# A two-layer RWKV-7 and S5 trunk: the bonus product is written over the receptance, and both pairs' bonus sums share one PSUM bank

## The chip, the cores and the metric

The kernel runs on one core of a Trainium2 chip. The metric is the device time of one execution in microseconds (us), as the median of the runs. The engines are named as in the profile: PE (matrix products), DVE (vector), ACT (scalar), POOL (GpSimd) and SP, which issues most of the DMAs.

## What is computed

The reference is a trunk of two layers over x of 1 x 1024 steps x 1024 features, float32. The first layer is RWKV-7 time mixing, the second an S5 state-space layer with a gated output; each is followed by a squared-ReLU MLP, and a LayerNorm stands after every part. The change lies in the first layer alone:

```python
r, k, v = xr @ wr, xk @ wk, xv @ wv
kk = k * k_k                      # per head, scaled to length 1
k = k * (1.0 + (a - 1.0) * k_a)
# per step of a head: state (64 x 64), decay w, o = state @ r
state = state * w + (state @ -kk) (kk * a)^T + v k^T
o = groupnorm(o) * lnx_g + lnx_b
bonus = sum(r * k * r_k, axis=-1) * v
out = ((o + bonus) * g) @ wo
```

The bonus is one number for each step and head, the sum over the head's 64 features of receptance times key times a weight `r_k`, by which the value `v` is scaled. There are 16 heads of 64 features.

## The kernel before

**Dense products.** The projections, the output product and the MLPs are written as three products of a high and a low part each (`mm3`, L257), with weights that stream from memory (L216 and L224 are their loads, L192 and L193 the split into parts). They take most of PE's time. Those of the second half of the steps and of the output run on PE between the products of the RWKV units.

**Units.** The recurrence is done in eight units of 256 steps and 512 features (8 heads), unit m in `elem(m)`. A unit has two pairs, j = 0 and 1, of two tiles of 128 features each. The steps form chunks of 64.

`elem` loads for a pair the key, the log decay `sg`, the rate `a` and the receptance `r` from DRAM scratch (L594; tiles `ldk`, `ldsg`, `lda`, `ldr`, each with two buffers, so that one pair's load takes the buffer that the same pair of the unit before has used). It sums squares for the norms (pss, L616, a power on POOL, a copy L621, transposes pn, L624, then the multiply into kk), runs a scan over `sg` (L629) and its exponentials E, builds the key `kf` (L638, L640; one buffer) and, on DVE, the operands of the unit's score products: AR from `r` and E (L643) and from kk (L644), KB from `kf`, `a` and `sg` (L648, L649).

Then POOL multiplies `kf` by `r` in place (L650). `bonus` takes four small products of it with the weights (pb, L654), in a bank of its own of the PSUM pool `pa`, and copies the sums out with two copies on DVE and two on ACT (L661). The pool `pa` has two banks, which hold pss, pn, the score blocks pA and the sums in turn. For j = 0 the sums stand behind the transposes pn of j = 1, for j = 1 behind the unit's last score product; an explicit order (`inorder`, L247) says so.

`amat` computes the score matrix in four blocks of eight products (pA, L687), each block in both banks of `pa`, and moves each to SBUF with a mask (AT, L691). `kbtrans` transposes KB (L702), `invert` inverts the chunk matrices (xa, x, xh, pv; L724 to L753, on DVE and PE by turns), `chain` runs the recurrence chunk by chunk (pR L796, its copy L798, pX L801, the copies to `vsa` on DVE L802 and ACT L803, pU L806, state L809 and L810, pO L815 and L817), and `gnorm` makes the output, with the copied sums `bo` as the bonus.

**Order.** The program is ordered by a list scheduler. Each part gets a rank (`core`), the scheduler has its own estimates of durations, and engines then run their instructions strictly in the order that comes out; while unit m runs its chain, unit m+1 runs `elem`, `amat` and `invert`. An instruction starts when the semaphores that it waits for are there, and everything behind it on its engine waits as well. A DMA issue on SP behaves in the same way.

Of the kernel before, what the change touches and what calls it, by code (L numbers as in the profile page):

```python
# [8 lines left out]
F32 = mybir.dt.float32  # L9
# [9 lines left out]
HT = 512  # L19
# [61 lines left out]
def trunk(ctx, tc, A):  # L81
    nc = tc.nc
    V, S, G, PE, SP = nc.vector, nc.scalar, nc.gpsimd, nc.tensor, nc.sync
# [8 lines left out]
    pa = ctx.enter_context(tc.tile_pool(name="pa", bufs=2, space=PSUM))  # L92
# [14 lines left out]
    ident = cp.tile([128, 128], F32, name="ident")  # L107
# [15 lines left out]
    def vec(n, k):  # L123
        i = PV.index(n)
        return pv[:, i, k : k + 1]
# [7 lines left out]
    rksel = kp.tile([128, KT, 2], F32, name="rksel")  # L133
# [113 lines left out]
    def inorder(prods):  # L247

        for x, y in zip(prods, prods[1:]):
            tc.add_manual_dep(y.ins, x.ins.name, mybir.DependencyInfo(  # L250
                mybir.DependencyClass.NoSync, mybir.DependencyReason.DATA), reason="order")
# [323 lines left out]
    NC, NP = 4, 4  # L575
# [7 lines left out]
    def elem(m):  # L583
        D = Unit()
        D.m, D.H, D.q, D.t0 = m, m // 4, m % 2, (m // 2) * 256
        D.KB, D.AR, D.o, D.vsa = [], [], {}, {}
        D.bo = kp.tile([128, NC, NP], F32, tag="bo", name="bo", bufs=3)
        D.PL = kp.tile([128, NC, NP], F32, tag="PL", name="PL", bufs=3)
        for j in range(2):
            n0 = 4 * D.q + 2 * j  # L590
            ld = {}
            for nm in ("k", "sg", "a", "r"):
                t = kp.tile([128, 512], F32, tag="ld" + nm, name="ld" + nm, bufs=EB[3] if nm in EB[4] else 1)
                SP.dma_start(t.rearrange("p (i t) -> p i t", i=2),  # L594
                             scr[nm][n0 * 128 : n0 * 128 + 256, D.t0 : D.t0 + 256].rearrange("(i p) t -> p i t", p=128))
                ld[nm] = t
            r, k, cs, a = ld["r"], ld["k"], ld["sg"], ld["a"]

            def v3(t):
                return t.rearrange("p (c l) -> p c l", l=L)  # L600

            def per(i):
                return slice(256 * i, 256 * i + 256)

            def ci(t):
                return t[:, :, 2 * j : 2 * j + 2].rearrange("p c i -> p i c")


            sq = kp.tile([128, HT], F32, tag="sq", name="sq", bufs=EB[0])
            kk = kp.tile([128, HT], F32, tag="kk", name="kk", bufs=EB[1])  # L610
            for i in range(2):
                S.mul(kk[:, per(i)], k[:, per(i)], vec("k_k", n0 + i))
            S.activation(sq, kk, AF.Square)
            ps = pa.tile([128, HT], F32, tag="a", name="pss")
            for tt in range(4):
                PE.matmul(ps[:, tt * 2 : tt * 2 + 2], sq[:, tt * 128 : (tt + 1) * 128], hsel, start=True, stop=True)  # L616
            rn = kp.tile([128, 8], F32, tag="rn", name="rn", bufs=2)
            V.tensor_scalar(rn, ps[:, 0:8], 1e-24, None, op0=ALU.max)
            G.tensor_tensor(rn, rn, mhalf[:, 0:8], op=ALU.pow)
            rnb = sq.rearrange("p (t h n) -> p t h n", t=4, h=2)  # L620
            S.copy(rnb, rn.rearrange("p (t h) -> p t h", h=2).unsqueeze(3).broadcast_to([128, 4, 2, 64]))  # L621
            pn = pa.tile([128, HT], F32, tag="a", name="pn")
            for tt in range(4):
                last = PE.transpose(pn[:, tt * 128 : (tt + 1) * 128], sq[:, tt * 128 : (tt + 1) * 128], ident)  # L624
            if j:
                D.bonus(last)
            V.tensor_mul(kk, kk, pn)

            V.tensor_tensor_scan(cs, cmask.rearrange("p c l -> p (c l)"), cs, 0.0, op0=ALU.mult, op1=ALU.add)  # L629
            E = kp.tile([128, 8, L + 1], F32, tag="E", name="E", bufs=EB[5])  # L630
            G.memset(E[:, :, 0:1], 1.0)
            S.activation(E[:, :, 1:], v3(cs), AF.Exp, scale=-DECAY)
            V.tensor_copy(ci(D.PL), E[:, :, L].rearrange("p (i c) -> p i c", i=2))
            S.activation(cs, cs, AF.Exp, scale=DECAY)

            kf = kp.tile([128, HT], F32, tag="kf", name="kf", bufs=EB[2])
            for i in range(2):
                S.activation(kf[:, per(i)], a[:, per(i)], AF.Identity, bias=kam[:, n0 + i : n0 + i + 1],  # L638
                             scale=kah[:, n0 + i : n0 + i + 1])
            G.tensor_mul(kf, kf, k)  # L640
            ar = kp.tile([128, 8, 2, L], F32, tag="AR", name="AR", bufs=ARB)
            kb = kp.tile([128, 8, 2, L], F32, tag="KB", name="KB", bufs=KBB)
            V.tensor_mul(ar[:, :, 1], v3(r), E[:, :, 1:])  # L643
            V.scalar_tensor_tensor(ar[:, :, 0], v3(kk), -1.0, E[:, :, 0:L], op0=ALU.mult, op1=ALU.mult)  # L644
            V.scalar_tensor_tensor(a, a, 1.0, kk, op0=ALU.add, op1=ALU.mult)
            for h in range(2):
                hs = slice(64 * h, 64 * h + 64)
                V.tensor_mul(kb[hs, :, 1 - h], v3(kf)[hs], v3(cs)[hs])  # L648
                V.scalar_tensor_tensor(kb[hs, :, h], v3(a)[hs], 0.5, v3(cs)[hs], op0=ALU.mult, op1=ALU.mult)  # L649
            G.tensor_mul(kf, kf, r)  # L650
            def bonus(after, kf=kf, n0=n0, j=j):
                pb = pa.tile([128, HT], F32, tag="a", name="pb")
                for tt in range(4):
                    prod = PE.matmul(pb[:, 2 * tt : 2 * tt + 2], kf[:, tt * 128 : (tt + 1) * 128], rksel[:, n0 + tt // 2],  # L654
                                     start=True, stop=True)
                    if tt == 0:
                        inorder([after, prod])
                pbv = pb[:, 0:8].rearrange("p (i c h) -> p c i h", i=2, c=2)
                for h in range(2):
                    for e in range(2):  # L660
                        (V.tensor_copy if e == 1 - h else S.copy)(  # L661
                            D.bo[64 * (1 - h) : 64 * (1 - h) + 64, e::2, 2 * j : 2 * j + 2],
                            pbv[64 * e : 64 * e + 64, :, :, h])

            D.bonus = bonus
            D.KB.append(kb)
            D.AR.append(ar)
        return D

    def amat(D):  # L670
# [7 lines left out]
        for j in range(2):  # L678
            for c2 in range(2):
                pp = [pa.tile([128, 2, 2, 128], F32, tag="a", name="pA") for h in range(2)]  # L680
                prods = []
# [8 lines left out]
                for h in range(2):  # L690
                    V.tensor_mul(at[:, h, 2 * c2 : 2 * c2 + 2, 2 * j : 2 * j + 2].rearrange("p c i j l -> p c i (j l)"),  # L691
                                 pp[h], amask.rearrange("p u j l -> p u (j l)").unsqueeze(1).broadcast_to([128, 2, 2, 128]))
        D.bonus(prods[-1])

    def kbtrans(D):
        D.kbt = {}
# [186 lines left out]
    def core():  # L883
# [6 lines left out]
        with rank(3000):  # L890
            cur = elem(0)
        with rank(5000):
            amat(cur)
            invert(cur)
# [800 lines left out]
    with rank(99100):  # L1695
        for k in range(4):
            a = t1[k]
# [104 lines left out]
```

## Time and profile before

| what | value |
|---|---|
| median of 3 runs | 2534.3 us (2532.02 to 2540.27) |
| profiled execution, device time | 2528.45 us |
| profiled execution, span of the trace | 2526.7 us |
| mean granted PE clock | 0.982 of full |
| POOL busy | 411.1 us (16%) |
| DMA, mean over the span | 135 GB/s |

The profile is that of one execution. Busy time is given for each engine; the chain of waits goes back from the last instruction to whatever released it; a row of a wait reads "engine, tile, line <- releaser: total, count, longest". The RWKV units run from about 75 to about 900 us of the span; the S5 layer and the MLPs fill the rest. POOL is the least busy of the engines in the table.

### The profile page before, as it was taken

The page shows a single profiled execution, that of the slowest core. Times are in us where ns is not written, and L with a number is a line of the kernel's source. Part 1 is how long each engine was busy: PE and PEld are TensorE (multiplying, and loading weights), DVE is VectorE, ACT ScalarE, POOL GpSimd, SP SyncE. Part 2 cuts the span into 40 slices and gives each one's busy share as a digit, 9 for nine tenths or more (in the row PEclk, how much of TensorE's full clock was granted, in tenths as well). Part 3 has the DMA queues.
Part 4 walks back from the last instruction along what each step waited for, and adds up shares of the span by engine and source line. Part 5 has one row for each costly group of instructions (what it writes and reads, how often), then busy time and mean ns, then how long its engine had stood idle before and what let it go on. Part 6 is the DMA issues. An engine that isn't in the chain of part 4 may idle for free.

```text
span 2526.7 us, 43006 instructions
## 1 busy us (share of the span) xinstructions
PE 2444.8 (97%) x16320; PEld 1996.6 (79%) x16320; DVE 1711.1 (68%) x3309; ACT 1217.3 (48%) x2197; POOL 411.1 (16%) x334
## 2 busy tenths in 40 slices
PE   9999889899899999999999999999999999999998
PEld 6788677688777878777788887887878888888887
DVE  7578787488795655997656475677666555655555
ACT  7655666454554444265445444434464333343434
POOL 3122332232231001021000000100232111111101
PEclk9999999999899999999999999999999999999998
DMA  5966555664223224444456565254351111111233
GB/s 177 311 214 206 166 188 159 209 185 132 70 78 97 90 84 147 130 132 119 131 178 192 170 248 187 92 190 144 114 170 58 54 48 55 47 54 51 87 112 114
DMA packets 217678, 340.60 MB, mean 135 GB/s; under 512 B 21248, under 2 KB 81792, under 8 KB 217472
## 3 DMA queue, kind: packets, MB, share of 16 engines
q1 hardware_dynamic: 216320, 335.77, 42.1%
q8 instruction: 128, 2.10, 0.4%
q10 hardware_dynamic: 1152, 2.10, 0.2%
q14 instruction: 78, 0.64, 0.1%
HBM read 267.53 MB, written 70.25 MB: 134 GB/s over the span
## 4 chain that ended last, share of the span: by engine, by line
PE 82%; DVE 8%; DMA 5%; ACT 3%; issue 1%; SPq 0%; POOL 0%; ACTq 0%; DVEq 0%; POOLq 0%
PE d L257 62%; PE d L1228 10%; PE pA L687 1%; DMA ldsg<-s_sg 1%; PE pk L1460 1%; DMA yl<-s_y 1%; PE pR L796 1%; PE pu L1499 1%; DVE wlo L193 1%; PE pbu L1511 1%; PE pU L806 0%; PE pO L817 0%; PE pX L801 0%; PE pO L815 0%; PE pq L952 0%
## 5 line engine op out<-in xcount | busy, mean ns | idle before, releaser
L193 DVE TENSOR_TENSOR wlo<-wraw,whi 128x512 fp32r<-128x512 f32 x424 | 314.3, 744 | 220.9 <-ACT whi L192 211.9
L192 ACT CAST whi<-wraw 128x512 fp32r<-128x512 f32 x424 | 261.8, 620 | 415.1 <-PE d L257 319.1
L257 PE MATMUL d<-qbuf,whi 128*128 128x512 f32 x1152 | 363.5, 397 | 6.5 <-ACT qbuf L192 3.3
L257 PE MATMUL d<-oAh,whi 128*128 128x512 f32 (+1 forms) x752 | 299.1, 405 | 8.4 <-ACT oAh L192 5.2
L257 PE MATMUL d<-oAl,whi 128*128 128x512 f32 (+1 forms) x752 | 297.1, 398 | 4.0 <-DVE oAl L960 4.0
L257 PE MATMUL d<-oAh,wlo 128*128 128x512 f32 (+1 forms) x752 | 297.3, 399 | 1.2 <-DMA wlo<-low 1.1
L257 PEld LDWEIGHTS d<-qbuf,whi 128*128 128x128 f32 x1152 | 213.5, 188 | 55.3 <-ACT qbuf L192 3.9
L257 PE MATMUL d<-qbuf,wlo 128*128 128x512 f32 x576 | 224.4, 394 | 0.0
L257 PE MATMUL d<-oBh,whi 128*128 128x512 f32 x496 | 195.6, 395 | 0.0
L257 PE MATMUL d<-oBh,wlo 128*128 128x512 f32 x496 | 195.0, 394 | 0.0
L257 PE MATMUL d<-oBl,whi 128*128 128x512 f32 x496 | 193.9, 391 | 0.0
L257 PEld LDWEIGHTS d<-oAh,whi 128*128 128x128 f32 (+1 forms) x752 | 141.7, 190 | 42.2 <-ACT oAh L192 5.5
L257 PEld LDWEIGHTS d<-oAl,whi 128*128 128x128 f32 (+1 forms) x752 | 141.5, 189 | 34.0 <-DVE oAl L960 4.5
L257 PEld LDWEIGHTS d<-oAh,wlo 128*128 128x128 f32 (+1 forms) x752 | 141.6, 189 | 32.4 <-DMA wlo<-low 1.6
L257 PE MATMUL d<-qh,whi 128*128 128x512 f32 x416 | 164.0, 394 | 0.0
L257 PE MATMUL d<-qh,wlo 128*128 128x512 f32 x416 | 163.1, 392 | 0.0
L257 PE MATMUL d<-ql,whi 128*128 128x512 f32 x416 | 161.6, 389 | 0.0
L257 PEld LDWEIGHTS d<-qbuf,wlo 128*128 128x128 f32 x576 | 108.5, 188 | 23.2
L257 PEld LDWEIGHTS d<-oBh,wlo 128*128 128x128 f32 x496 | 93.1, 188 | 21.5 <-issue 0.6
L257 PEld LDWEIGHTS d<-oBl,whi 128*128 128x128 f32 x496 | 93.1, 188 | 21.4 <-issue 0.7
L257 PEld LDWEIGHTS d<-oBh,whi 128*128 128x128 f32 x496 | 93.2, 188 | 19.7 <-issue 0.5
L1287 DVE TENSOR_TENSOR hA<-hA,d 128x512 f32<-128x512 f32 x104 | 71.4, 686 | 48.2 <-PE d L257 48.1
(499 smaller groups left out, 5208.9 us busy)
## 6 DMA issues: line engine op xcount, KB each, us to landing
wraw<-in_mw_dram SPq DMA_DIRECT2D x356, 256.0 KB, 2.8
wlo<-low SPq DMA_DIRECT2D x92, 256.0 KB, 3.1
wraw<-in_glu_dram SPq DMA_DIRECT2D x64, 256.0 KB, 2.8
low<-wlo SPq DMA_DIRECT2D x52, 256.0 KB, 4.1
raw<-in_mw_dram SPq DMA_DIRECT2D x52, 256.0 KB, 2.7
wraw<-in_wk_dram SPq DMA_DIRECT2D x32, 256.0 KB, 4.3
wraw<-in_wr_dram SPq DMA_DIRECT2D x32, 256.0 KB, 4.3
wraw<-in_wv_dram SPq DMA_DIRECT2D x32, 256.0 KB, 5.0
```

Source lines behind the costliest of these rows:

```text
L192: S.copy(hi, src)
L193: op = (e or V).tensor_sub(lo, src, hi.bitcast(F32))
L257: bulk.append((PE.matmul(p, w, x, **kw).ins, x.shape[-1]))
L687: prods.append(PE.matmul(pp[h][:, cc, i], D.KB[j][hs, u].rearrange("p j l -> p (j l)"), D.AR[j][hs, u].rearrange("p j l -> p (j l)"), star ...
L796: hop.append(PE.matmul(pR[hs, i], at[:, h, c, i, 0], vsa[:, cl, h, i], start=True, stop=True))
L1228: PE.matmul(p, w[:, k], x, start=not add and k + j == 0, stop=k == 3 and j == 2, skip_group_check=True)
L1287: V.tensor_add(z, z, p)
L1460: PE.matmul(p[64 * par : 64 * par + 16, g2], bb[ps_, ri, 4 * f + g2], ca[ps_, g2, ri, 0:8].rearrange("p t c -> p (t c)"), start=ri == 0, s ...
L1499: PE.matmul(p[64 * (1 - e) : 64 * (1 - e) + 64, g], u1[j][:, g].rearrange("p s c -> p (s c)"), sel[:, e], start=True, stop=True)
L1511: PE.matmul(p[qs, ri, g2], tb[:, g2, ri, qs], u[:, 2 * g2 + par], start=True, stop=True)
```

## The change

The multiply on POOL now writes into the tile of `r` instead of that of `kf`, and stands right behind the first AR product, which is the other reader of `r`. `elem` makes no sums any more. At the end of `amat`, behind the last score product, one bank takes all eight sums of the unit, those of both pairs, and four copies of 64 x 8 numbers move them out, in place of two times four copies of 64 x 4. The number of small products is the same, and so is what `gnorm` reads.

```diff
-        D.KB, D.AR, D.o, D.vsa = [], [], {}, {}
+        D.KB, D.AR, D.rk, D.o, D.vsa = [], [], [], {}, {}
...
-                last = PE.transpose(pn[:, tt * 128 : (tt + 1) * 128], sq[:, tt * 128 : (tt + 1) * 128], ident)
-            if j:
-                D.bonus(last)
+                PE.transpose(pn[:, tt * 128 : (tt + 1) * 128], sq[:, tt * 128 : (tt + 1) * 128], ident)
...
             V.tensor_mul(ar[:, :, 1], v3(r), E[:, :, 1:])
+            G.tensor_mul(r, kf, r)
+            D.rk.append(r)
...
-            G.tensor_mul(kf, kf, r)
-            def bonus(after, kf=kf, n0=n0, j=j):
-                pb = pa.tile([128, HT], F32, tag="a", name="pb")
-                for tt in range(4):
-                    prod = PE.matmul(pb[:, 2 * tt : 2 * tt + 2], kf[:, tt * 128 : (tt + 1) * 128], rksel[:, n0 + tt // 2],
-                                     start=True, stop=True)
-                    if tt == 0:
-                        inorder([after, prod])
-                pbv = pb[:, 0:8].rearrange("p (i c h) -> p c i h", i=2, c=2)
-                for h in range(2):
-                    for e in range(2):
-                        (V.tensor_copy if e == 1 - h else S.copy)(
-                            D.bo[64 * (1 - h) : 64 * (1 - h) + 64, e::2, 2 * j : 2 * j + 2],
-                            pbv[64 * e : 64 * e + 64, :, :, h])
...
-        D.bonus(prods[-1])
+        pb = pa.tile([128, HT], F32, tag="a", name="pb")
+        sums = [PE.matmul(pb[:, 8 * j + 2 * tt : 8 * j + 2 * tt + 2], D.rk[j][:, tt * 128 : (tt + 1) * 128],
+                          rksel[:, 4 * D.q + 2 * j + tt // 2], start=True, stop=True) for j in range(2) for tt in range(4)]
+        inorder([prods[-1], sums[0]])
+        pbv = pb[:, 0:16].rearrange("p (i c h) -> p c i h", i=NP, c=2)
+        for h in range(2):
+            for e in range(2):
+                (V.tensor_copy if e == 1 - h else S.copy)(D.bo[64 * (1 - h) : 64 * (1 - h) + 64, e::2],
+                                                          pbv[64 * e : 64 * e + 64, :, :, h])
```

Lines up to L641 keep their numbers but for one or two; AR's first product is L641 in the changed program, pA L671, the sums L678, their copies L684, and from pT (L694) on each line is 8 lower than before.

The scheduler makes another order from this. The first place is PE at the score products of unit 2, in the stretch where unit 1 runs its chain (a row "x8" is eight products in a row; `d` is a dense product). Before:

```order
L796 MATMUL pR<-vsa,AT_2641 64x64 x8
L654 MATMUL pb<-rksel,kf 128x2
L687 MATMUL pA<-AR,KB 128x128
L654 MATMUL pb<-rksel,kf 128x2 x3
...
L801 MATMUL pX<-o,XT 64x64 x8
L687 MATMUL pA<-AR,KB 128x128 x7
L806 MATMUL pU<-vsa,kbt 64x64 x8
```

The same place in the changed program:

```order
L793 MATMUL pX<-o,XT 64x64 x8
...
L671 MATMUL pA<-AR,KB 128x128 x8
...
L671 MATMUL pA<-AR,KB 128x128
...
L671 MATMUL pA<-AR,KB 128x128 x7
...
L798 MATMUL pU<-vsa,kbt 64x64 x8
L807 MATMUL pO<-st,AR 64x64 x8
L809 MATMUL pO<-vsa,AT_2627 64x64 x8
L678 MATMUL pb<-rksel,ldr 128x2 x8
L616 MATMUL pss<-hsel,sq 128x2 x4
```

The first sums have left their place among the score products, all eight now stand together, and 21 dense products stand between pX and pU, where none stood (the marks "..." there are dense products).

The second place is DVE where unit 4's score matrix ends and unit 5's first pair begins. Before:

```order
L629 SCALAR_TENSOR_TENSOR ldsg<-cmask,ldsg 128x512
...
L633 COPY PL<-E 128x2x4
L643 TENSOR_TENSOR AR<-ldr,E 128x8x64
L661 COPY bo<-pb 64x2x2 x2
...
L793 COPY vsa<-st 64x256
L724 STREAM_TRANSPOSE xa<-x_6596 128x1024
L837 TENSOR_REDUCE sm<-o 128x8
L661 COPY bo<-pb 64x2x2 x2
L618 TENSOR_SCALAR rn<-pss 128x8
```

And now, with unit 5's AR in it:

```order
L675 TENSOR_TENSOR AT<-pA,amask 128x2x256 x2
L618 TENSOR_SCALAR rn<-pss 128x8
L641 TENSOR_TENSOR AR<-ldr,E 128x8x64
L716 STREAM_TRANSPOSE xa<-x_6571 128x1024
L684 COPY bo<-pb 64x2x4 x2
L193 TENSOR_TENSOR oAl<-m,oAh 128x512
L794 COPY vsa<-pX 64x256
```

AR, which reads the freshly loaded `ldr`, now stands ahead of the transpose, of unit 4's sums' copies and of the copy to `vsa` that the chain needs. On PE the rows at this place read:

```order
L678 MATMUL pb<-rksel,ldr 128x2 x8
L616 MATMUL pss<-hsel,sq 128x2 x4
L793 MATMUL pX<-o,XT 64x64 x8
...
L624 MATMUL pn<-ident,sq 128x128 x4
...
L798 MATMUL pU<-vsa,kbt 64x64 x8
```

Between pX and pn stand 16 dense products of half width, and 8 more between pn and pU.

The third place is SP's queue, with the semaphores that each issue waits for. Before, a load of `r` waited for POOL:

```order
L216 DMA wraw_5661<-in_wv_dram 128x512 [waits DMAHW7_49]
L594 DMA ldsg_6777<-s_sg_130 128x2x256 [waits DMAHW0_49,DVE_49]
L594 DMA lda_6779<-s_a_131 128x2x256 [waits DMAHW1_49]
L594 DMA ldr_6781<-s_r_128 128x2x256 [waits DMAHW2_49,Pool_49]
L216 DMA wraw_5691<-in_wv_dram 128x512 [waits DMAHW3_49]
```

Now such a load waits for PE:

```order
L457 DMA s_r_128<-ev_5509 128x512 [waits DMAHW6_49,Activation_49]
L224 DMA wlo_5674<-low37_1859 128x512 [waits DMAHW7_49,PE_49]
L594 DMA ldr_6756<-s_r_128 128x2x256 [waits DMAHW0_49,PE_49]
L216 DMA wraw_5799<-in_wv_dram 128x512 [waits DMAHW1_49,Activation_49]
L457 DMA s_r_128<-ev_5512 128x512 [waits DMAHW2_49,Activation_49]
```

It no longer follows the loads of `sg` and `a` directly, and weights and stores stand behind it. All differences of order lie in about the first 900 us of the program.

More of the change, by code (lines that the diff above doesn't have):

```diff
@@ L649, in elem @@
                 V.scalar_tensor_tensor(kb[hs, :, h], v3(a)[hs], 0.5, v3(cs)[hs], op0=ALU.mult, op1=ALU.mult)
-            G.tensor_mul(kf, kf, r)
-            def bonus(after, kf=kf, n0=n0, j=j):
-                pb = pa.tile([128, HT], F32, tag="a", name="pb")
-                for tt in range(4):
-                    prod = PE.matmul(pb[:, 2 * tt : 2 * tt + 2], kf[:, tt * 128 : (tt + 1) * 128], rksel[:, n0 + tt // 2],
-                                     start=True, stop=True)
-                    if tt == 0:
-                        inorder([after, prod])
-                pbv = pb[:, 0:8].rearrange("p (i c h) -> p c i h", i=2, c=2)
-                for h in range(2):
-                    for e in range(2):
-                        (V.tensor_copy if e == 1 - h else S.copy)(
-                            D.bo[64 * (1 - h) : 64 * (1 - h) + 64, e::2, 2 * j : 2 * j + 2],
-                            pbv[64 * e : 64 * e + 64, :, :, h])
-            D.bonus = bonus
             D.KB.append(kb)
```

## The prediction

> **What bounds the kernel now.** I read the page's table of engines first, then the slices of the granted clock, then the chain of waits.
>
> ```profile
> PE 2444.8 (97%) x16320; PEld 1996.6 (79%) x16320; DVE 1711.1 (68%) x3309; ACT 1217.3 (48%) x2197; POOL 411.1 (16%) x334
> PEclk9999999999899999999999999999999999999998
> PE 82%; DVE 8%; DMA 5%; ACT 3%; issue 1%; SPq 0%; POOL 0%; ACTq 0%; DVEq 0%; POOLq 0%
> ```
>
> TensorE is busy for 97% of the span and is 82% of the chain that ended last. A change that touches no dense product can only win what PE idles, or what it runs below full clock. The windows of 100 us show where that is.
>
> ```profile
> core 0: us, PE busy (x) PEld busy (x) DVE busy (x) ACT busy (x) POOL busy (x), PEclk, DMA share, GB/s
> 300.00:400.00 100.00, 86.80 (x827) 69.17 (x828) 77.56 (x186) 64.43 (x126) 30.58 (x25) 0.93 0.64 205
> 600.00:700.00 100.00, 90.58 (x878) 73.60 (x873) 83.57 (x187) 47.47 (x89) 26.34 (x21) 0.90 0.23 71
> 900.00:1000.00 100.00, 100.00 (x816) 79.85 (x815) 53.92 (x108) 40.81 (x75) 12.70 (x10) 1.00 0.34 100
> ```
>
> In the stage of the RWKV units PE idles 13.2 and 9.4 us in the two stretches shown, and runs at 0.93 and 0.90 of its clock; past 900 us it idles not at all. So the change is decided inside the units, by waits of PE. These five, from the view of PE's waits (total, count, longest, in us), are those that the change can touch:
>
> ```profile
> PE pA L687 <- ACT bo L661: 6.0, 2, 5.1
> PE pv L745 <- DVE x L738: 5.6, 2, 4.5
> PE pA L687 <- DVE AT L691: 3.9, 2, 3.6
> PE pb L654 <- POOL kf L650: 1.9, 2, 1.5
> PE pb L654 <- DVE AT L691: 1.2, 1, 1.2
> ```
>
> The first is the change's target: a block of score products waits for a bank of `pa` until the copies of the sums have emptied it. The timeline shows how the 5.06 us came about (start, duration, engine, line, operation, count, and in brackets the wait ahead of it):
>
> ```profile
> 299.07 0.68 PE L801 MATMUL pX<-o,XT 64*64 64x64 f32 x16
> 302.69 1.23 DVE L629 TENSOR_TENSOR_SCAN ldsg<-cmask,ldsg 128x512 f32<-128x512 f32 x1 [2.61 <-DMA ldsg<-s_sg]
> 303.94 0.33 DVE L661 COPY bo<-pb 64x4 f32<-64x4 f32 x2
> 304.31 0.43 DVE L802 COPY vsa<-pX 64x256 f32<-64x256 f32 x1
> 304.60 0.16 ACT L661 COPY bo<-pb 64x4 f32<-64x4 f32 x1
> 304.78 0.37 ACT L803 COPY vsa<-pX 64x256 f32<-64x256 f32 x1
> 304.81 2.08 PE L687 MATMUL pA<-AR,KB 64*128 64x128 f32 x14 [5.06 <-ACT bo L661]
> ```
>
> The copies were late because DVE stood in front of a scan whose `sg` load had not landed; the bank was the way in which that reached PE. Three more such waits of DVE for `sg` reached PE, the first of them twice (488.80 and 494.31); the view of DVE's waits gives the totals:
>
> ```profile
> 488.80 0.71 PE L687 MATMUL pA<-AR,KB 64*128 64x128 f32 x8 [0.98 <-ACT bo L661]
> 494.31 0.79 PE L687 MATMUL pA<-AR,KB 64*128 64x128 f32 x2 [3.55 <-DVE AT L691]
> 501.52 0.38 PE L257 MATMUL d<-whi,oAl 128*128 128x256 f32 x1 [1.41 <-DVE oAl L193]
> 563.58 1.92 PE L745 MATMUL pv<-x,AT 32*32 32x32 f32 x64 [4.54 <-DVE x L738]
> DVE ldsg L629 <- DMA ldsg<-s_sg: 27.3, 10, 6.1
> DVE AR L643 <- DMA ldr<-s_r: 7.8, 4, 2.7
> ```
>
> PE's stalls behind `sg` waits are 5.06 + 0.98 + 3.55 + 1.41 + 4.54 = 15.5 us, for 27.3 us that DVE waited: 0.57 us of PE for one of DVE. I use that ratio for every new wait of DVE in this stage.
>
> **What the bank wait's end is worth.** With both pairs' sums behind the last score product, no score product of the same unit waits for a bank with sums. At 304.81 that does not give back all of 5.06 us: in the old order pU follows the block, and pU needs L803's copy, which ends at 305.15 (304.78 + 0.37). The block's 2.08 us would have been done by 302, so pU would be the next one to wait: about 2.1 us are sure. But the new order also puts 21 dense products between pX and pU there. Two neighbours of a full-width run give their interval:
>
> ```profile
> 486.29 0.39 PE L257 MATMUL d<-oAh,whi 128*128 128x512 f32 x1
> 486.52 0.39 PE L257 MATMUL d<-oAl,whi 128*128 128x512 f32 x1
> 300.00:310.00 10.00, 5.19 (x63) 4.62 (x63) 7.20 (x14) 6.33 (x13) 3.49 (x3) 0.52 0.80 255
> 160.00:170.00 10.00, 8.26 (x54) 7.86 (x53) 9.74 (x22) 6.47 (x13) 4.37 (x3) 0.83 0.60 176
> ```
>
> 21 x 0.23 = 4.8 us of cover, nearly the whole stall. Between 2.1 and 5.1 I take 4.0, nearer the upper end because the cover is in the order. The 0.98 us at 488.80 goes too (1.0). The 1.9 us in which the sums waited for Pool's product go, since the sums now come after all four blocks (1.9); the 1.2 us behind AT stay. The window 300 to 310 ran at 0.52 of the clock, so its 5.19 busy us hold 0.48 x 5.19 = 2.5 us of lost clock, which go with the stall. Gain: 4.0 + 1.0 + 1.9 + 2.5 = 9.4 us, with bounds of 6 (2.1 for the stall, half of the clock) and 10.5.
>
> [...]
>
> **The copies and the buffer of kf.** 32 of the 64 copies go, 16 on each of DVE and ACT, at
>
> ```profile
> L661 ACT COPY bo<-pb x32: 155/159/165, 121.5 to 867.6; 64x4 f32<-64x4 f32 x32
> L648 DVE TENSOR_TENSOR KB<-kf,ldsg x32: 670/686/1694, 76.6 to 751.7; 64x512 f32<-64x512 f32 x32
> ```
>
> 16 x 0.159 = 2.5 us on each engine over eight units: off the path, beside dense products, 0 for the end; at most 2.5 x 0.57 = 1.4 us. `kf` (one buffer) comes free at the KB products instead of at the sums, so the next pair's `kf` may start earlier; no wait of PE in the view names that buffer, so I price it at 0. Pool's multiply now waits for AR alone, not for the readers of `kf`; what is queued behind it on Pool (the next pair's memset, `kf` product and power) comes no later than before: 0.
>
> **The cost: who holds r now.** `ldr` has two buffers, one for each pair. Before, Pool's multiply was the last reader. Now the product lies in the buffer until the sums are done on PE, at the end of the unit's score matrix; only then may the next unit's `r` be fetched. The load's price is in its issue row (ns) and its time from issue to landing (us):
>
> ```profile
> L594 SPq DMA_DIRECT2D ldr<-s_r x16: 359/370/1409, 93.6 to 669.9; - x16
> DMA to landing us min/median/max: 2.7/3.9/6.0
> L643 DVE TENSOR_TENSOR AR<-ldr,E 128x512 f32<-128x512 f32 x16 | 10.9, 683 | 10.1 <-DMA ldr<-s_r 10.1
> L724 DVE STREAM_TRANSPOSE xa<-x 128x1024 f32<-128x1024 f32 x8 | 16.2, 2025 | 7.3 <-ACT x L723 7.2
> L193 DVE TENSOR_TENSOR oAl<-m,oAh 128x512 fp32r<-128x512 f32 x40 | 31.2, 791 | 2.5 <-ACT oAh L192 2.3
> ```
>
> 0.37 + 3.9 = 4.3 us from the sums to a usable `r`. In the new order DVE has, between the sums' copies and the next unit's first AR, one scan and one product of this size (1.23 + 0.68 = 1.9), two scans or so (2.6), one scan (1.2), and at three places 1.5, nothing and nothing. So DVE stands 2.4, 1.7, 3.1, 2.8, 4.3 and 4.3 us at six of the seven places: 18.6 us.
>
> One of those, from unit 4 to 5, I work out directly, since the order puts AR and the transpose ahead of the sums' copies and all of them ahead of vsa. From the sums on: r 4.3, AR 0.68, xa 2.03, two copies 0.33, oAl 0.79, L802 0.43 and ACT's L803 0.37, together 8.9 us until pU may run. PE has meanwhile, in the new order, the norm sums, pX, 24 half-width products (12 x 0.23 = 2.8) and four transposes. Their rows, with the copy between sums and transposes:
>
> ```profile
> 212.34 1.03 PE L616 MATMUL pss<-hsel,sq 128*128 128x2 f32 x8
> 215.87 0.61 ACT L621 COPY sq<-rn 128x512 f32<-128x512 f32 x1
> 217.76 0.66 PE L624 MATMUL pn<-ident,sq 128*128 128x128 f32 x4
> ```
>
> 1.03 + 0.68 + 2.8 + 0.66 = 5.2 us, so PE stalls about 3.7 us, and with clock at the first stall's rate (2.5 for 5.06) 1.8 more: 5.5. It is 0 if DVE arrives late at AR, and up to 8.9 if the dense products have been run early.
>
> The other five make 14.3 us of DVE, x 0.57 = 8.2 of PE; the waits for `r` that exist now (7.8 x 0.57 = 4.4) are not paid twice: 3.8 net. Bounds: -4.4 (none of it reaches PE) and 9.9 (all of it does).
>
> Last, the chain from norm sums to transposes takes at least 215.87 + 0.61 - 212.34 = 4.1 us; at two places the new order has some 2.0 and 2.5 us of PE work in between, where no place of the old one had under 3.4. The shortfall is 3.7 us; some of it is taken by waits already counted, so 2.0, between 0 and 3.7.
>
> Behind a load that waits, SP's queue holds back the weights and stores issued after it.
>
> ```profile
> SPq L216 <- DVE wlo L193: 782.9, 297, 10.6
> ```
>
> SP already waits 782.9 us over the span for weight buffers, in 297 waits of this kind of up to 10.6 us, under a PE that is 97% busy, so I take 0; above, one late weight load of 4.3 us.
>
> **The sum.** -9.4 + 5.5 + 3.8 + 2.0 = +1.9 us. The profiled execution took 2528.45 us (span 2526.7), 5.9 us under the median of 2534.3 of the three runs, which spread from 2532.02 to 2540.27. As a difference the sum goes onto the median: 2536. A step of 0.3%, 7.6 us, is about what a measurement of this kernel can tell from no change.
>
> **Rivals.** *A, faster: r is hidden.* DVE is busy for 84 us of 100 around 650 us; if it reaches AR later than the order suggests, `r` has landed and only the gains stay: -9.4, about 2525. For it: only 4 waits for `r` exist now. Against: the `sg` loads, freed by KB and thus before the sums, are already awaited 10 times. Chance 0.27.
>
> *B, slower: r just in time.* Each of the waits for `r` reaches PE one for one and takes clock with it at 0.49 of the stall. Against my sum: the net of the five places is 9.9 instead of 3.8 (+6.1), with clock 4.9, and the gain of the first stall shrinks to its sure 2.1 (+1.9): 1.9 + 12.9 = +14.8, about 2549. It decides when more than about three quarters of DVE's waits reach PE. For it: at 563.58 one wait of DVE alone cost PE 4.54 us; against: the mean of 0.57. Chance 0.24.
>
> *C, slower: Pool and DVE disturb each other.* Pool's multiply no longer waits for the KB products of its own pair and may run beside them. The KB row runs from 0.686 (median) to 1.694 us, so something already slows one. If one KB product in each of 16 pairs goes from the median to the longest, 16 x 1.008 = 16 us of DVE, x 0.57 = 9 us: about 2545. [...] Chance 0.07.
>
> That the sums do not in fact stand together is excluded by the order.
>
> **Numbers.** My forecast, no change that can be told, has 0.42; faster is A's 0.27; slower is B's and C's 0.31. The forecast's own range, from the bounds of its terms, is 2529 to 2542. Eight in ten needs most of both sides: 2521 to 2550.
>
> **What would show it.** Right: no wait of pA for `bo`; DVE's waits at AR for `ldr` rising from 7.8 toward 18 to 20 us; a wait of pU or pn of 2 to 5 us near unit 4's end; the windows from 100 to 800 us as idle as before. A is right if the waits for `ldr` stay under 8 us. B shows as PE waits on vsa, x or AT behind AR of together over 10 us more, with the clock below 0.9 in their windows. C shows in the KB group's mean well above 0.7 us. I am wrong if the time changes outside 100 to 900 us, where the order is the same.

## The result and the profile after

The changed kernel takes 2524.32 us (median of 9 runs, 2519.7 to 2532.25), the one before 2536.56 us (9 runs, 2530.68 to 2540.27). The ratio is 0.9957, with a 95% interval of 0.9945 to 0.997: faster by 0.43%, where the forecast was no change (2536).

The profiled execution of the changed kernel took 2532.25 us (span 2530.5), the slowest of its nine runs; that of the kernel before, with 2528.45 us, was among the fastest of its own. Laid side by side these two say that the change is slower. So both kernels were profiled a second time (below, with the experiments); the rows read here are of the first profile of after, and its second profile has the four largest waits of PE within 1 us of these. The page of the profile after has the same three lines at its top:

```profile
PE 2451.0 (97%) x16320; PEld 2000.3 (79%) x16320; DVE 1718.6 (68%) x3293; ACT 1211.4 (48%) x2181; POOL 406.2 (16%) x334
PEclk9999999999899999999999999999999999999998
PE 82%; DVE 9%; DMA 4%; ACT 3%; issue 2%; POOL 0%; SPq 0%; ACTq 0%; DVEq 0%; POOLq 0%
```

The same bound, then, with 16 copies less on DVE and 16 on ACT. The three windows shown of before:

```profile
core 0: us, PE busy (x) PEld busy (x) DVE busy (x) ACT busy (x) POOL busy (x), PEclk, DMA share, GB/s
300.00:400.00 100.00, 89.88 (x812) 69.89 (x813) 78.77 (x182) 63.60 (x123) 32.26 (x25) 0.88 0.64 201
600.00:700.00 100.00, 90.34 (x848) 74.58 (x848) 83.02 (x185) 45.67 (x87) 26.36 (x20) 0.90 0.25 77
900.00:1000.00 100.00, 100.00 (x818) 80.13 (x817) 54.06 (x108) 41.10 (x76) 12.71 (x11) 1.00 0.33 98
```

PE still idles 10.1 and 9.7 us in the two stretches of the unit stage, and not at all in the one behind it. The waits of PE between 60 and 900 us have no row left of pA for `bo` and none of pb; the largest are now these:

```profile
PE d L257 <- DVE oAl L193: 10.0, 6, 2.8
PE d L257 <- ACT ev L472: 5.6, 2, 5.3
PE pX L793 <- ACT o L790: 4.3, 3, 1.8
PE pA L671 <- DVE AT L675: 3.7, 3, 2.2
```

The second of them is the surprise. It stands at the place of the 5.06 us stall that was to go (timeline, with the wait in brackets):

```profile
300.14 0.68 PE L793 MATMUL pX<-o,XT 64*64 64x64 f32 x16
305.39 1.26 ACT L472 ACTIVATE ev<-d,pvh 128x512 f32<-128x512 f32 x2 [6.02 <-DMA s_sg<-ev]
306.13 1.37 PE L257 MATMUL d<-oAh,whi 64*128 64x512 f32 x2 [5.31 <-ACT ev L472]
308.95 0.43 DVE L794 COPY vsa<-pX 64x256 f32<-64x256 f32 x1
```

The score products no longer wait for a bank with sums, but the dense products that now stand there wait 5.31 us for a bank of their own, which ACT empties late, since its target `ev` waits for an earlier store to land. The stall changed its name and kept its length; in the second profile of after it is 5.5 us.

The cost that I had feared did not come. DVE's waits between 100 and 800 us:

```profile
DVE ldsg L627 <- DMA ldsg<-s_sg: 23.1, 11, 4.9
DVE AR L641 <- DMA ldr<-s_r: 6.9, 5, 3.7
```

6.9 us for `r` instead of 7.8, not 18 to 20 (in the second profiles 6.5 us, against 5.5 before). The timeline shows why, from unit 4 to 5 and, behind the mark, from unit 5 to 6 (an SPq row is the issue of a load):

```profile
500.97 1.95 PE L678 MATMUL pb<-rksel,ldr 128*128 128x2 f32 x16
502.05 0.37 SPq L594 DMA_DIRECT2D ldr<-s_r  x1
503.85 0.17 DVE L618 TENSOR_SCALAR rn<-pss 128x8 f32<-128x8 f32 x1 [3.23 <-PE pss L616]
505.56 1.07 PE L793 MATMUL pX<-o,XT 64*64 64x64 f32 x16 [1.76 <-ACT o L790]
505.88 0.69 DVE L641 TENSOR_TENSOR AR<-ldr,E 128x512 f32<-128x512 f32 x1 [1.87 <-DMA ldr<-s_r]
507.14 0.58 PE L257 MATMUL d<-whi,oAh 128*128 128x256 f32 x1 [0.50 <-ACT oAh L192]
509.53 0.58 PE L257 MATMUL d<-whi,oAl 128*128 128x256 f32 x1 [1.17 <-DVE oAl L193]
510.25 0.36 ACT L795 COPY vsa<-pX 64x256 f32<-64x256 f32 x1
...
587.83 1.84 PE L678 MATMUL pb<-rksel,ldr 128*128 128x2 f32 x16
588.80 1.26 SPq L594 DMA_DIRECT2D ldr<-s_r  x2
593.30 0.69 DVE L641 TENSOR_TENSOR AR<-ldr,E 128x512 f32<-128x512 f32 x1
```

The load is issued 1.0 to 1.1 us after the first of the sums has begun, as soon as the first pair's four are done, and not after all of them. And DVE gets to AR late: at 593.30 it does not wait at all (the two loads there land 2.7 and 2.8 us after their issue), and at 505.88 it waits 1.87 us, until 3.83 us after the issue has begun at 502.05. SP does stand for the sums, but no row of PE's waits between 60 and 900 us names a load:

```profile
SPq L594 <- PE pb L678: 17.4, 8, 9.1
```

### The profile page after: what moved, and what is told of

The parts are those of the page before. It is cut to its first block, busy times and chain, and to the rows that moved or that the text cites. A ratio compares the mean times of both kernels' runs of the same rounds, so it can differ in the third digit from the quotient of the medians.

```text
span 2530.5 us, 42967 instructions
## 1 busy us (share of the span) xinstructions
PE 2451.0 (97%) x16320; PEld 2000.3 (79%) x16320; DVE 1718.6 (68%) x3293; ACT 1211.4 (48%) x2181; POOL 406.2 (16%) x334
## 4 chain that ended last, share of the span: by engine, by line
PE 82%; DVE 9%; DMA 4%; ACT 3%; issue 2%; POOL 0%; SPq 0%; ACTq 0%; DVEq 0%; POOLq 0%
PE d L257 61%; PE d L1220 10%; PE pA L671 1%; DVE wlo L193 1%; PE pk L1452 1%; PE pu L1491 1%; DMA ldr<-s_r 1%; PE pR L788 1%; PE pbu L1503 1%; PE pU L798 1%; PE pq L944 1%; PE pO L809 1%; PE pO L807 1%; DVE KB L648 1%; PE pX L793 1%
```

## The experiments

The runs are told in the order in which they were made; each ratio is to runs of the kernel before in the same series. The scheduler makes another order of the whole unit stage from the smallest edit, so a second kind of kernel was made: `hold` adds, at the end of the program, a dependency without a semaphore from each instruction of an engine to the next one of a list. That fixes the engine's order and adds no wait for another engine; copies8_held below, which has this addition, is as fast as the kernel whose order it takes (0.9953 beside 0.9957).

```python
for packed in ORDER:                  # one list of instruction numbers per engine
    at, last = 0, None
    for step in zlib.decompress(base64.b85decode(packed)).split():
        at += int(step)
        ins = by.get(f"I-{at}")
...
        if last is not None:
            tc.add_manual_dep(ins, last, mybir.DependencyInfo(
                mybir.DependencyClass.NoSync, mybir.DependencyReason.DATA), reason="order")
        last = ins.name
```

The theories, by the names that the expectations use. *Place*: the gain is that no score product stands behind sums. *One bank*, *copies*: it is the shared bank, or the 32 copies saved. *Buffer*: `kf` comes free early and POOL waits less. *Freedom*: the same, but through orders that it allows. *Order*: any new order of this size moves the time by some us, and the changed kernel drew a good one.

### One half each

**after_again** is the changed kernel once more.

> The changed kernel once more, unaltered: a second profile and a second interval. All theories: 0.9957 of the kernel before, within 0.9945 and 0.997, some 2525 us. In its trace the waits of DVE at AR for ldr stay near 10 us in all between 60 and 900 us (9.7 in the first profile), and no wait of pA for bo appears. If the waits for ldr were near 20 us here, the first profile was no good witness against the cost that I had forecast.

Measured: 0.996 (0.9945 to 0.9974), 2526.09 us; DVE waits 9.5 us for `ldr` between 60 and 900 us (9.7 in the first profile). That the wait for `r` did not grow is confirmed.

**r_only** has the product in `r`, the sums at their old places:

```diff
+            G.tensor_mul(r, kf, r)
...
-            G.tensor_mul(kf, kf, r)
-            def bonus(after, kf=kf, n0=n0, j=j):
+            def bonus(after, kf=r, n0=n0, j=j):
```

> Only the first half of the change: the product goes into the buffer of r right behind AR, but each pair's sums stay at their old places, in a bank of their own, with eight copies a unit. Theory 'place' (the gain is that the sums left the middle of the score products): no gain, 1.000 within 0.002, 2536 us, with pA waiting for bo and pb for POOL as before (together some 5 to 8 us). Theory 'buffer' (the gain is that kf comes free early and POOL no longer waits for KB): all of the gain, 0.996. Theory 'order' (any new order of this size moves the time by some us): anything from 0.996 to 1.004.

Measured: 0.9964 (0.9951 to 0.9977). All of the gain, without any move of the sums. But in this order PE has no wait of pA for `bo` and none of pb either, so this run alone does not tell *place* from *order*; that is left to the runs below.

**two_banks** gives each pair's sums a bank of their own at the end:

```diff
+        for j in range(2):
+            pb = pa.tile([128, HT], F32, tag="a", name="pb")
+            sums = [PE.matmul(pb[:, 2 * tt : 2 * tt + 2], D.rk[j][:, tt * 128 : (tt + 1) * 128],
...
```

> The change, but each pair's four sums take a bank of their own behind the last score product, with eight copies a unit in all, as many as before. Theory 'place': the gain stays, 0.996 (2526 us), since no score product of the unit follows. Theory 'one bank' (it is the shared bank that pays, as the second bank stays free for the next norm sums): most of the gain is gone, 0.999. Theory 'copies': gone as well, 1.000. Theory 'order': anything from 0.992 to 1.000.

Measured: 1.0019 (1.0008 to 1.003). **copies8** empties the one bank by eight copies:

```diff
+                for j in range(2):
+                    (V.tensor_copy if e == 1 - h else S.copy)(
+                        D.bo[64 * (1 - h) : 64 * (1 - h) + 64, e::2, 2 * j : 2 * j + 2],
+                        pbv[64 * e : 64 * e + 64, :, 2 * j : 2 * j + 2, h])
```

> The change with its one bank, but emptied with eight copies of 64 x 4 a unit instead of four of 64 x 8, as many as before. The 32 copies take 16 x 0.16 = 2.6 us more on each of DVE and ACT. Theory 'copies': the gain is mostly gone, 0.999 to 1.000 of the kernel before. Theory 'place' and theory 'one bank': 0.996 to 0.997, at most 1.4 us slower than the changed kernel. Theory 'order': anything from 0.992 to 1.000.

Measured: 1.0011 (0.9999 to 1.0023). Taken alone, these two runs say that the bank and the copies are the whole gain, while r_only has the gain with neither. That does not go together easily, unless it is the order.

### The order held

**before_again** is the kernel before once more.

> The kernel before, unaltered: a second profile, since the first (2528.45 us) is one of its fastest runs. All theories: 1.000, some 2536 us. Theory 'stalls' (the time of a variant is PE's idle time plus lost clock up to the end of the units): idle time and lost clock of PE over the first 1100 us come to about 98 us here, against 92 in the first profile, 97 and 93 in the two profiles of the changed kernel and 88 for the product in r alone.

Measured: 1.000 (0.9988 to 1.0013), 2536.3 us; idle time and lost clock of PE in the first 1100 us, added up over eleven windows of 100 us (idle, and busy time x (1 - PEclk)), are 56.5 + 47.0 = 103.5 us, a little more than expected. The wait that the change removes is smaller here than in the first profile of before: the longest of pA for `bo` is 2.1 us, not 5.1.

```profile
PE pA L687 <- ACT bo L661: 2.9, 2, 2.1
```

**swap_b** exchanges the copies' engines in the kernel before:

```diff
-                        (V.tensor_copy if e == 1 - h else S.copy)(
+                        (S.copy if e == 1 - h else V.tensor_copy)(
```

> The kernel before with an edit that should be worth nothing: the four copies of a pair's sums change engines (the two on DVE go to ACT and the other way round), with the same number on each. The scheduler makes another order from it. Theory 'order' (any new order moves the time by some us): off 1.000 by 0.002 to 0.005, either way. Theory 'place', theory 'buffer' and theory 'copies': 1.000 within 0.0015.

Measured: 1.0011 (0.9999 to 1.0023): as *place*, *buffer* and *copies* had it, and less than *order* had said.

**r_only_held** is the product in `r` in the old order of PE, DVE, ACT and POOL (`G.tensor_mul(r, kf, r)` in the old line, and `hold`).

> The product goes into the buffer of r, the sums stay at their old places, and PE, DVE, ACT and POOL keep the kernel before's order, instruction by instruction; only SP's order is the scheduler's, as loads of r must come later. The product in r alone, in an order of its own, gave 0.9964. Theory 'buffer' in its strong form (kf and POOL simply wait less): most of the gain is here too, 0.997. Theory 'order' and theory 'freedom' (the free buffer pays only through an order that it allows): no gain, 1.000 to 1.003, slower where the loads of r come late for the old order.

Measured: 1.004 (1.0027 to 1.0053). Without its new order the product in `r` costs 0.4%, so *buffer* in its strong form falls. The waits of DVE for `ldr` between 60 and 900 us, here and, below it, in before_again:

```profile
DVE AR L643 <- DMA ldr<-s_r: 14.6, 6, 3.8
```

```profile
DVE AR L643 <- DMA ldr<-s_r: 8.1, 5, 3.2
```

**copies8_held** is copies8 in the changed kernel's order, each copy replaced by two neighbours.

> The change with eight copies of 64 x 4 a unit instead of four of 64 x 8, and with every engine's order held as in the changed kernel, each copy replaced by two neighbours. In an order of its own this edit gave 1.0011, as if the copies were worth 0.5%. Theory 'copies': 1.001 again. Theory 'order': the gain stays, 0.996 to 0.997, as 32 copies of 0.16 us are worth at most 1.4 us; the 0.5% were then the new order's.

Measured: 0.9953 (0.9936 to 0.997). The copies are worth nothing; the same instructions in copies8's own order had taken 1.0011. This is the first pair of runs that differ in the order alone.

### Which part of the old order's loss, and more orders

**late_load_b** is the kernel before, all engines held, with SP's order from r_only_held.

> The kernel before, its product in kf, with PE, DVE, ACT and POOL in its own order; only the loads of r stand as late in SP's queue as with the product in r and the old order, which gave 1.004. It has that kernel's order on every engine, and none of its loads of r waits for PE. Theory 'late load' (the 1.004 is r landing late for an order that was made for an early r): 1.003 to 1.004, with DVE's waits at AR for ldr near 14 us. Theory 'queue' (the 1.004 is SP standing still with weights and stores behind a load that waits for sums): 1.000 to 1.001.

Measured: 1.0032 (1.002 to 1.0045), and DVE waits as *late load* said:

```profile
DVE AR L643 <- DMA ldr<-s_r: 13.7, 8, 2.9
```

So a late `r` does cost some 8 us, in an order that was made for an early one. DVE's waits for it grow by 5.6 us, and PE's idle time over the first 1100 us by 8.8 (65.3 against 56.5 in before_again); by which waits of PE was not followed. What the product in `r` and SP's standing still add in the same order (1.004 against 1.0032) is within the intervals.

**swap_a**, **swap_r** and **swapj_b** exchange the copies' engines in the changed kernel, in r_only, and (for the second pair alone) in the kernel before; the edit is that of swap_b, and for swapj_b `(e == 1 - h) == (j == 0)` in place of `e == 1 - h`.

> The changed kernel with the edit that should be worth nothing: the four copies of a unit's sums change engines. The scheduler makes another order. In the kernel before the same edit gave 1.0011. Theory 'place' (sums behind the score products pay in any order): 0.996 within 0.0015. Theory 'order' (the gain belongs to one order that came out well): anywhere from 0.994 to 1.002.

> The product in r alone, sums at their old places, with the copies' engines exchanged: another order of the kernel that gave 0.9964. Theory 'freedom' (a kf that is free early lets the scheduler make better orders as a rule): 0.996 within 0.0015. Theory 'order': anywhere from 0.994 to 1.002.

> The kernel before with the copies' engines exchanged for the second pair alone: a third order of the kernel before, after 1.000 (its own) and 1.0011 (both pairs exchanged). Theory 'freedom' and theory 'place': 1.000 to 1.002, as no order of the kernel before reaches the gain. Theory 'order': anywhere from 0.995 to 1.003.

Measured: swap_a 0.9993 (0.9978 to 1.0007), swap_r 0.9938 (0.992 to 0.9955), swapj_b 0.9988 (0.9979 to 0.9998). An edit that should be worth nothing takes the changed kernel's gain away, although the sums stand behind the score products and no wait of pA for `bo` is left: *place* falls. swap_r, with 2518.68 us, is the fastest version of this study.

**hpat_b**, **hpat_a**, **hpat_r** choose the copies' engines by head (`V.tensor_copy if h else S.copy`) in the kernel before, in the changed one and in r_only; **swapj_r** is swapj_b's edit in r_only.

> The kernel before with the copies' engines chosen by head: DVE takes both copies of one head, ACT both of the other. A fourth order of the kernel before, after 1.000, 1.0011 and 0.9988. Theory 'order': as wide as the orders of the changed kernel, so 0.996 to 1.003 is possible. Theory 'freedom' (the old program has no good order, because kf holds the next pair back): 0.9985 to 1.0015.

> The changed kernel with the copies' engines chosen by head. A further order of the changed kernel, after 0.9957 (its own), 0.9993 (exchanged) and 1.0011 (eight copies). Theory 'order': anywhere from 0.995 to 1.002, on the average 0.999. Theory 'place': 0.996.

> The product in r alone, sums at their old places, the copies' engines chosen by head: a third order of that program after 0.9964 and 0.9938. Theory 'freedom': 0.993 to 0.997 again. Theory 'order' (those two were lucky): nearer 1.000, 0.998 or above.

> The product in r alone, sums at their old places, the copies' engines exchanged for the second pair: a fourth order of that program. Theory 'freedom': 0.993 to 0.997. Theory 'order': 0.998 or above in this or in the other new order.

Measured: hpat_b 0.9954 (0.9942 to 0.9967), hpat_a 0.9966 (0.995 to 0.9982), hpat_r 1.0038 (1.0021 to 1.0054), swapj_r 0.9984 (0.9972 to 0.9995). The kernel before reaches the whole gain without the change, and r_only loses it: *freedom* falls. The engines by head are no gain in themselves either, since hpat_r is the slowest of its program. hpat_b reaches it with both things that I had held to be decisive still in it, the waits of pA for the sums' bank and those of AR for `r` (between 60 and 900 us):

```profile
PE pA L687 <- DVE bo L661: 6.7, 2, 4.9
```

```profile
DVE AR L643 <- DMA ldr<-s_r: 15.4, 5, 7.3
```

### Two programs, instruction for instruction

**before_reordered** is the kernel before, held to hpat_b's order on every engine; **after_reordered** is the changed kernel, held to copies8's.

> The kernel before, every instruction as it was, held on all engines to the order of the kernel before with engines chosen by head, which gave 0.9954. Theory 'order': 0.9954 within 0.0015, that is all of the change's gain (0.9957) without the change. Theory 'the edit pays': 1.000, since nothing of the edit is in it; the 0.9954 would then be the copies' engines.

> The changed kernel, every instruction as it is, held on all engines to the order that the scheduler made for its version with eight copies, which gave 1.0011. Theory 'order': 1.0011 within 0.002, the whole gain gone with the change in place. Theory 'the edit pays' (place, one bank, r): 0.996 to 0.997.

Measured: after_reordered 1.0008 (0.9994 to 1.0022), as *order* had it: the change is in place, instruction for instruction, and its gain is gone. before_reordered 1.0029 (1.0018 to 1.0041), against 0.9954 for hpat_b in the same order, and against my expectation. The waits of ACT over the whole span show the difference, in before_reordered, then in before_again:

```profile
ACT bo L661 <- DVE bo L661: 29.5, 16, 5.6
ACT bo L661 <- PE pb L654: 8.0, 5, 3.0
```

```profile
ACT bo L661 <- PE pb L654: 6.6, 5, 1.8
ACT bo L661 <- DVE bo L661: 4.2, 4, 2.1
```

In the kernel before, ACT's second copy of a pair can wait until DVE's two are done, though it reads and writes other numbers (interleaved columns of the same rows); in hpat_b no row of this wait exists. Its order has ACT reach its copies early, and makes ACT stand for DVE in all 16 pairs here. The longest of these waits holds back PE as well (timeline of before_reordered):

```profile
294.52 0.16 ACT L661 COPY bo<-pb 64x4 f32<-64x4 f32 x1
300.31 0.16 ACT L661 COPY bo<-pb 64x4 f32<-64x4 f32 x1 [5.64 <-DVE bo L661]
```

```profile
300.52 2.07 PE L687 MATMUL pA<-AR,KB 64*128 64x128 f32 x14 [5.43 <-ACT bo L661]
```

But the same block stalls in hpat_b too, behind DVE's copies:

```profile
299.24 2.04 PE L687 MATMUL pA<-AR,KB 64*128 64x128 f32 x14 [4.86 <-DVE bo L661]
```

So this place makes 0.6 of the 19 us between the two runs, and that ACT's 29.5 us make the rest is not shown. What is shown is that an order that is good for one set of dependencies is not good for another: hpat_b's 0.9954 is the order together with four copies that don't tie the engines to each other. How the two share it was not tried.

### All orders side by side

| program | orders made by the scheduler: ratio to the kernel before |
|---|---|
| before, with its engine edits | 1.000, 1.0011, 0.9988, 0.9954 |
| product in `r`, sums at the old places | 0.9964, 0.9938, 0.9984, 1.0038 |
| changed, with its engine edits | 0.9957, 0.9993, 0.9966 |
| changed, with eight copies, or two banks | 1.0011, 1.0019 |

The means of the first three rows are 0.9988, 0.9981 and 0.9972, and 0.9989 for the changed kernel with the fourth row counted in; within each of the first three rows the orders lie 0.4% to 1% apart. Of so few orders no row can be told from another. The engine edits also change which copies wait for which, so the rows are not the order alone; the pairs with every instruction the same are, and they differ by 0.29% (before_reordered and the kernel before), 0.5% (after_reordered and the changed kernel) and 0.58% (copies8 and copies8_held).

Where the time differs is seen in the start of the first products behind the units (pk, the first of the two times in a row; before_again, after_again, swap_r and hpat_r, in this order):

```profile
L1460 PE MATMUL pk<-ca,bb x256: 269/269/280, 1099.4 to 1417.9; 64*16 64x128 f32 x128
```

```profile
L1452 PE MATMUL pk<-ca,bb x256: 267/270/281, 1089.4 to 1408.5; 64*16 64x128 f32 x128
```

```profile
L1460 PE MATMUL pk<-ca,bb x256: 266/269/280, 1084.8 to 1404.2; 64*16 64x128 f32 x128
```

```profile
L1460 PE MATMUL pk<-ca,bb x256: 269/269/280, 1105.5 to 1423.8; 64*16 64x128 f32 x128
```

From there to the end of the span (2535.5, 2524.6, 2521.2, 2542.1) it is 1436.1, 1435.2, 1436.4 and 1436.6 us, the same. All of it has come about before. There PE's idle time and lost clock, worked out as for before_again, are 56.5 + 47.0, 52.2 + 40.5, 55.9 + 30.9 and 58.3 + 51.7 us. Their sums, 103.5, 92.7, 86.8 and 110.0, rank as these four times do; and more than half of each difference from the first is the clock, not the idle time.

One profile of each is thin for that: the first profiles of before and after have 59.8 + 31.8 and 54.4 + 43.2 us, idle time within 3.3 us of the second profiles, but lost clock 15 us lower and 3 us higher. The idle time is 5.5 and 4.3 us lower in after in the two pairs of profiles. For the clock, the mean over all runs of a series is better: 0.9768 for the kernel before against 0.9790 for after_again, 0.9771 against 0.9830 for swap_r, 0.9768 against 0.9739 for hpat_r. Times the span these are, by estimate, 6 of the 10 us that after_again gains, all of swap_r's 14 and 7 of the 11 that hpat_r loses.

## Why the prediction was wrong

**The side was wrong, and the step that failed is what the sum leaves out.** I priced the waits that I could name at their places and set the rest of the new order at nothing, without a reason, although the order shows that all engines run differently up to 900 us. That rest is worth as much as the whole result: copies8_held against copies8, 0.58%, and after_reordered against the changed kernel, 0.5%, with not an instruction different. Of the terms that are in the sum, the rise of the wait for `r` (+9.3) did not come, and the gain at the bank (-9.4) is not shown to have come as reckoned. Rival A gave the right figure (2525) and half of the right reason: `r` is hidden, its waits stay under 8 us as A had said (6.9 between 100 and 800 us), but the gains are not those that it kept, so that the figure fits is partly luck. The range was also narrower than its own terms: their bounds add up to 2519 to 2551 us, not to 2529 to 2542, and the measured 2524 lies inside the former.

**The bank wait (-9.4).** The wait for `bo` is gone in the changed kernel, but the gain at its place is not: PE stalls 5.31 us there on another bank. The cover that I counted, 21 dense products, is itself what waits. Nor was the wait typical: in the second profile of before it is 2.05 us long at that place, and hpat_b is fast with 6.7 us of it. Of the 9.4 us nothing is shown to have been won as I said. The sure part was worked out too high as well: pU began at 304.81 + 2.08 = 306.89 and could have begun at 305.15, so 1.7 us, not 2.1.

**Copies, `kf`, POOL, SP (0).** The copies: right, by copies8_held. `kf` and POOL: right in the old order, where r_only_held, with the product in `r`, is no faster than late_load_b without it. SP's queue: it waits 17.4 us for the sums without a row of PE's waits that names a load; r_only_held lies 0.08% above late_load_b, which the intervals do not tell from nothing.

**The wait for r (+5.5 and +3.8).** At the one place that I worked out directly DVE waits 1.87 us for `r`, not 4.3, and `vsa` is complete 510.25 + 0.36 - (500.97 + 1.95) = 7.7 us after the end of the sums, not 8.9. The stall that I forecast, pU waiting 3.7 us for `vsa`, does not come: pU starts 3.2 us after `vsa` is there, without a wait.

```profile
513.85 0.69 PE L798 MATMUL pU<-vsa,kbt 128*64 128x64 f32 x16
```

PE does stall there, 1.76 + 0.50 + 1.17 = 3.4 us in all, but that this is near 3.7 is luck: only the 1.17 stand behind AR on DVE (through the transpose, the copies and oAl); the other two wait for ACT, for a copy and a split that read nothing of `r`. Over all places DVE waits 6.9 us between 100 and 800 us, not 18.6. I had started the load's 4.3 us at the end of the sums and let DVE arrive at AR as if its queue were empty; it starts 1.0 to 1.1 us after the first sum, and where DVE does not wait at all (593.30), it had been busy for 3.16 of the 3.3 us before. In the old order the term is real (0.3% to 0.4%); in the new one AR stands late enough to hide most of it.

**Norm sums (+2.0).** No wait of pn for the copied norms is among PE's rows of after; before_again has 1.9 us of them. Wrong in sign.

**Rivals B and C.** B's mechanism shows where the order is kept, and there its price is 8 to 10 us (late_load_b 1.0032, r_only_held 1.004), not 15. What C said shows too, but small. In the first profile of after three of the 32 KB products of `kf` start while POOL's multiply runs and take 1.66 to 1.76 us instead of 0.69 (in the first profile of before one product of KB with `a` does, 1.68 us); the first of these places in after (the two products take 0.68 and 1.70 us), then the group in before_again and in after_again (busy time, mean in ns):

```profile
107.21 2.38 DVE L648 TENSOR_TENSOR KB<-kf,ldsg 64x512 f32<-64x512 f32 x2
107.42 1.62 POOL L642 TENSOR_TENSOR ldr<-kf,ldr 128x512 f32<-128x512 f32 x1 [2.78 <-issue]
```

```profile
L648 DVE TENSOR_TENSOR KB<-kf,ldsg 64x512 f32<-64x512 f32 x32 | 23.9, 747 | 1.2 <-ACT ldsg L634 0.9
L648 DVE TENSOR_TENSOR KB<-kf,ldsg 64x512 f32<-64x512 f32 x32 | 25.9, 809 | 4.2 <-PE pT L694 3.0 <-ACT ldsg L632 0.9
```

That is three times 1.0 us, 3 us of DVE in the first profile of after, and not 16, and the time fell all the same; what it costs by itself was not tried.

**The clock.** I let a stall cost half its length in clock (1.8 us for the stall behind `r`), by the one window of the first stall (2.5 for 5.06). PE's three longest kinds of wait in before_again between 60 and 900 us:

```profile
PE pv L745 <- DVE x L738: 6.5, 2, 4.9
PE d L257 <- ACT oAh L192: 6.3, 3, 2.7
PE d L257 <- DVE oAl L960: 4.4, 1, 4.4
```

These are six waits, 17.2 us in all, and the lost clock is 47.0 us in the same profile beside 56.5 us of idle time, more than half: my rule was an estimate from one stall and was not worked through to that figure. Nor does the idle time of a stretch settle its clock. In the first profile of the kernel before PE has two waits near 162 us, 1.00 and 0.74 us long; the clock is 0.50 in the windows of 1 us from 164 to 167 us, and the stretch from 160 to 170 runs at 0.83 with 1.74 us idle; in before_again, with the same order, it runs at 1.00 with 2.46:

```profile
160.00:170.00 10.00, 7.54 (x56) 6.64 (x54) 9.74 (x23) 6.84 (x14) 4.64 (x3) 1.00 0.53 182
```

So this stretch lost clock in one execution and none in the other, which idled longer there, and over the first 1100 us two executions of one kernel lost 31.8 and 47.0 us of clock: in part that is chance. Which stall sets off which drop, if one does, was not separated.

What stays open: which of an order's many short waits make it good, why some orders keep a higher clock on the mean (0.9830 for swap_r, 0.9771 for the kernel before), and what the move of the sums is worth by itself with the order held. That was not tried: with `r` kept until the unit's last sums, the old order has the next unit's AR ahead of the very sums that it must wait for. Averaged over orders, the edit is nothing that these runs can tell.

## What to carry to other kernels

Where a scheduler writes the order, an edit's time is the edit and one draw from the orders that it can lead to; here the draws lie 0.4% to 1% apart, as much as the change or more. Before a gain of that size is put down to an edit, make two or three edits that should be worth nothing, or hold the order and change the work, and see whether the gain stays. A wait that goes at one place is won only if the next thing in the queue there can run (here 5.06 us behind one bank became 5.31 us behind another), so look at what its banks and buffers wait for.

## What was not expected of the hardware

Two executions of the same kernel differ by up to 17 us within one series (2525.01 to 2541.72 for the kernel before), and one profile of each kernel pointed the wrong way. The granted clock fell to 0.50 from 164 to 167 us in one execution of the kernel before (0.83 over the stretch from 160 to 170, with 1.74 us idle) and was 1.00 over the same stretch in another, with 2.46 us idle. Two halves of one little copy job on two engines can hold each other: 29.5 us of ACT's time in 16 pairs of copies of 0.16 us, 4.2 us in the order of the kernel before; that is a wait for a semaphore of the program, and not shown to be a trait of the engines. A KB product of `kf` on DVE took 1.66 to 1.76 us instead of 0.69 where it started while POOL's multiply ran, three times in the first profile of after.
